# A conv-FFN encoder's last down projections: every second tile summed in a pair bank, eight PSUM banks in place of four

## The chip, the cores and the metric

The kernel runs on one core of one Trainium2 chip. The metric is the device time of one execution in microseconds (us). Three runs of the kernel before took 1843.85 to 1846.6 us, with a median of 1845.19.

The engines are named as in the profile: PE is TensorE (matmuls; PEld are its weight loads), DVE is VectorE, ACT is ScalarE, POOL is GpSimd, SP is SyncE, which issues the transfers. PSUM, in which TensorE sums its results, has eight banks; a [128, 512] tile of 32-bit floats fills one.

## The reference

Two sequences, a prompt of 256 tokens and a sample of 512, go through the same trunk of two layers, D = 1024. The kernel treats them as one array of 768 columns, prompt first.

```python
for l in range(2):
    h = rmsnorm(x, norm_g[l, 0]) * (1 + sc1) + sh1
    y = mlstm_mixer(h, ...) if l == 0 else swa_mixer(h, ...)   # sliding-window attention in layer 1
    x = x + g1 * y
    h = rmsnorm(x, norm_g[l, 1]) * (1 + sc2) + sh2
    x = x + g2 * conv_ffn(h, ffn_w_up[l], ffn_conv_w[l], ffn_conv_b[l], ffn_w_down[l])
return rmsnorm(x, final_g)

def conv_ffn(h, w_up, conv_w, conv_b, w_down):
    u = h @ w_up                          # 1024 -> 2 x 2816
    u = depthwise_conv3(u) + conv_b
    g, val = u[..., :2816], u[..., 2816:]
    return (silu(g) * val) @ w_down       # 2816 -> 1024
```

All in 32-bit floats. sh, sc and g come from a condition vector for each sequence.

## The kernel before

**Layout.** Activations lie transposed, channels on the 128 partitions and tokens along the columns. The residual x is eight row blocks c = 0 to 7 of 128 channels, held in two tiles (slab_4542 and slab_4543 in layer 0). A 32-bit product is made from three reduced-precision products: each operand is split into a high part (written by ScalarE, L260) and a low part (by VectorE, L261), and TensorE adds w_high x a_high, w_high x a_low and w_low x a_high; `mm` (L254) issues each of the three. In the names of the profile a weight's parts are whi and wlo, an activation's zh and zl.

**The conv-FFN.** `ffn` runs over NPART = 11 parts of 256 hidden channels. `up(p)` makes the part's up projection as pairs (`pair`, matmuls at L1169, L1170, L1172), which use a fixed set of four PSUM banks, `self.bank[0]` to `self.bank[3]` (tiles named ps), and ScalarE and VectorE take the results out of them (L1182, L1223, L1229, L1240, L1242, L1243). Convolution and gate follow (L1387, L1389, L1390, L1397, L1402). `down(p, g)` is issued after `up(p + 1)`: part 9's down projection stands behind the pairs of part 10, and part 10's behind nothing. So the pairs are over when the last two down projections run.

**A down tile.** `tile(w, c, rng)` makes one row block c for one range of columns: two chunks of 128 hidden channels, three matmuls each, six matmuls summed in one bank; then `resid` (L590, VectorE) reads the bank and adds it, scaled, to x. Parts 0 to 9 go over each half of the weights (c 0 to 3, then 4 to 7), and in it over the sample's 512 columns and the prompt's 256, four row blocks each: 16 tiles. Part 10 goes over three ranges of 256 columns (two of the sample, then the prompt), eight row blocks each: 24 tiles. Each tile takes its bank from `pa()`, a pool of four banks that are handed out in turn (tiles named pa); a bank is written again only when VectorE's L590 has read it.

**The norm behind part 10.** After each range the next norm begins: `square` (L111, ScalarE) of every x block, sums of the squares (L115, on POOL in layer 0 and on VectorE in layer 1), a matmul with `inv` that sums over partitions (the pm tile; in the last range of layer 1 the squares are summed by matmuls at L129), L152 or L150, a power on POOL (L153), and a matmul with `kct` (the pr tile) that spreads the factor over the partitions. Then `apply`: in layer 0 `modulated`, which makes the next layer's zh and zl (L549 on VectorE, L551 on ScalarE, L552 on VectorE) for the attention's projections; in layer 1 `output` (L574, L578, L579, L581) and the store of the result (L582). Beside it, the first projections of layer 1's attention already run on the ranges that are ready; L868 (ScalarE) and L870 (VectorE) take the first heads' results out of the ps banks, L895 and L896 others'.

**What sets the order.** The instructions of each engine are put in order by a scheduler, which lays the program out on a timeline of its own when it is built. The order of the code sets priorities, not positions. Which bank a tile has is therefore an input of the order: an instruction that would wait for a bank is placed behind others that would not. The banks of `pa()` are handed out in that scheduled order, the fixed banks by the code.

`ps()` hands out the four fixed banks in turn:

```python
def ps(self):
    if self.bank is None:
        return self.pb.tile([P, 512], F32, tag="ps", name=self.nm("ps"), bufs=4)
    self.turn += 1
    return self.bank[self.turn % 4]

def pa(self):
    return self.psp.tile([P, 512], F32, tag="pa", name=self.nm("pa"), bufs=4)
```

## Time and profile before

| | |
|---|---|
| median of three runs | 1845.19 us (1843.85 to 1846.6) |
| the profiled execution | 1843.78 us, with a span of 1842.0 us from first to last instruction |
| mean granted TensorE clock | 0.994 |
| TensorE busy | 1793.2 us, 97% of the span |
| VectorE busy | 1367.0 us, 74% |
| ScalarE busy | 895.3 us, 49% |
| POOL busy | 488.0 us, 26% |
| layer 0: parts 9 and 10 of the down projection | about 994 to 1042 us |
| layer 1: parts 9 and 10 of the down projection | about 1785 to 1832 us |

Times in the profile are counted from the start of the span. A row of the timeline gives start, duration, engine, line, operation, out<-in, sizes, count, and in brackets how long the engine had been idle and what it waited for. A row of the view of waits gives total, number and longest wait. A row of the view of windows gives each engine's busy time in a stretch, and the mean clock that TensorE was granted in it. Matmuls overlap, so a listed matmul lasts longer than the distance to the next one.

### The profile page before, as it was taken

Reading aid. Unit: us, or ns where it says so; the run is one execution under the profiler, and the core shown is the slowest. Engines: PE = TensorE matmul, PEld = TensorE weight load, DVE = VectorE, ACT = ScalarE, POOL = GpSimd, SP = SyncE. Lnnn points to the kernel's source line nnn. Section 1 sums busy time; section 2 is a strip of 40 time slices with the busy share of each in tenths; the row PEclk is TensorE's granted clock in tenths of the full one; section 3 lists DMA queues with packets and bytes.
Section 4 is the critical chain, followed back from the end, with each engine's and each line's share of the span. In section 5 each row is a group of like instructions: output and inputs, shape, how many; then the busy total and the mean of one; then the engine's idle time right before and its main releaser. Section 6 shows DMA issues by size and latency. Waiting matters only on the chain.

```text
span 1842.0 us, 28931 instructions
## 1 busy us (share of the span) xinstructions
PE 1793.2 (97%) x11290; PEld 1657.4 (90%) x11290; DVE 1367.0 (74%) x2101; ACT 895.3 (49%) x1815; POOL 488.0 (26%) x386
## 2 busy tenths in 40 slices
PE   6999999999999999999999999999999999999997
PEld 3987887889998999999999999889989999999997
DVE  4755676886689877777777757766898777777776
ACT  4443443354456444444444556765564444444443
POOL 1001001021024333333331313430144333333322
PEclk9999999999999999999999999999999999999999
DMA  8344566546312221222223321124122222222212
GB/s 330 119 145 134 172 195 221 164 138 219 101 46 74 76 61 66 69 69 69 69 69 93 104 83 50 53 94 129 50 86 69 69 69 69 69 69 70 69 35 69
DMA packets 64245, 184.48 MB, mean 100 GB/s; under 512 B 6167, under 2 KB 23831, under 8 KB 64108
## 3 DMA queue, kind: packets, MB, share of 16 engines
q1 hardware_dynamic: 64108, 182.63, 30.8%
q8 instruction: 89, 1.46, 0.3%
q14 instruction: 48, 0.39, 0.1%
HBM read 176.17 MB, written 6.43 MB: 99 GB/s over the span
## 4 chain that ended last, share of the span: by engine, by line
PE 86%; DVE 6%; DMA 3%; ACT 2%; issue 1%; POOL 1%; SPq 0%; POOLq 0%; ACTq 0%; DVEq 0%
PE ps L254 27%; PE pa L254 25%; PE ps L1169 10%; PE ps L1172 10%; PE ps L1170 10%; PE pa L1008 1%; DMA slab<-in_adaln_w_dram 1%; DMA raw<-in_w_dram 1%; DVE wlo L261 1%; DVE ada L506 1%; DVE slab L590 1%; DMA raw<-in_adaln_w_dram 0%; PE pa L1172 0%; PE pa L1169 0%; PE pa L1170 0%
## 5 line engine op out<-in xcount | busy, mean ns | idle before, releaser
L260 ACT CAST whi<-raw 128x1024 fp32r<-128x1024 f32 x237 | 247.9, 1048 | 350.4 <-PE pa L254 161.4
L261 DVE TENSOR_TENSOR wlo<-raw,whi 128x1024 fp32r<-128x1024 f32 x237 | 316.6, 1337 | 119.8 <-ACT whi L260 117.3
L254 PE MATMUL pa<-slab,whi 128*128 128x256 f32 (+1 forms) x1472 | 346.6, 331 | 3.2 <-DVE slab L590 3.2
L254 PEld LDWEIGHTS pa<-slab,whi 128*128 128x128 f32 x1472 | 252.7, 188 | 27.5 <-DVE slab L590 4.5
L590 DVE SCALAR_TENSOR_TENSOR slab<-pa,mod,slab 128x256 f32<-128x256 f32 (+1 forms) x368 | 211.2, 592 | 70.8 <-PE pa L254 70.5
L254 PE MATMUL pa<-slab,wlo 128*128 128x256 f32 (+1 forms) x736 | 233.9, 330 | 0.0
L254 PE MATMUL ps<-zh,whi 128*128 128x256 f32 (+1 forms) x560 | 189.0, 339 | 2.3 <-ACT whi L260 1.7
L254 PE MATMUL ps<-zh,wlo 128*128 128x256 f32 (+1 forms) x560 | 184.1, 330 | 2.0 <-DVE wlo L261 2.0
L254 PE MATMUL ps<-zl,whi 128*128 128x256 f32 (+1 forms) x560 | 185.1, 332 | 0.0
L1169 PE MATMUL ps<-zh,whi 128*128 128x384 f32 x504 | 172.3, 342 | 3.6 <-ACT nt L1240 1.8
L1170 PE MATMUL ps<-zl,whi 128*128 128x384 f32 x504 | 169.9, 337 | 0.8 <-DVE zl L1126 0.8
L1172 PE MATMUL ps<-zh,wlo 128*128 128x384 f32 x504 | 168.9, 335 | 0.0
L254 PEld LDWEIGHTS pa<-slab,wlo 128*128 128x128 f32 x736 | 138.5, 188 | 13.1 <-DVE wlo L261 0.4
L1205 POOL TENSOR_TENSOR raw<-raw,raw 128x512 f32<-128x512 f32 x40 | 52.2, 1305 | 330.8 <-DVE wlo L261 259.4
L254 PE MATMUL ps<-slab,whi 128*128 128x384 f32 x512 | 132.0, 339 | 0.9 <-DVE slab L261 0.5
L1402 POOL TENSOR_TENSOR slab<-slab 128x772 f32<-128x772 f32 x44 | 86.5, 1967 | 164.6 <-DVE slab L1390 152.7
L1389 DVE SCALAR_TENSOR_TENSOR slab<-slab,cstt,slab 128x771 f32<-128x771 f32 x88 | 103.6, 1179 | 26.6 <-ACT slab L1387 26.5
L254 PEld LDWEIGHTS ps<-zh,whi 128*128 128x128 f32 x560 | 107.4, 192 | 15.9 <-issue 4.4
L506 DVE SCALAR_TENSOR_TENSOR ada<-raw,silc,ada 128x1024 f32<-128x1024 f32 x84 | 110.6, 1354 | 14.9 <-DMA raw<-in_adaln_w_dram 14.8
L1202 POOL TENSOR_TENSOR raw<-raw 128x512 f32<-128x512 f32 x40 | 68.5, 1712 | 200.1 <-DMA raw<-in_w_dram 169.7
L254 PEld LDWEIGHTS ps<-zh,wlo 128*128 128x128 f32 x560 | 107.2, 192 | 12.2 <-DVE wlo L261 2.9
L254 PEld LDWEIGHTS ps<-zl,whi 128*128 128x128 f32 x560 | 107.4, 192 | 11.9 <-issue 3.4
(291 smaller groups left out, 4265.7 us busy)
## 6 DMA issues: line engine op xcount, KB each, us to landing
raw<-in_w_dram SPq DMA_DIRECT2D x208, 512.0 KB, 3.7
raw<-in_adaln_w_dram SPq DMA_DIRECT2D x84, 512.0 KB, 4.6
slab<-in_x_dram SPq DMA_DIRECT2D x12, 512.0 KB, 6.8
slab<-in_adaln_w_dram SPq DMA_DIRECT2D x12, 512.0 KB, 10.3
slab<-mrows SPq DMA_DIRECT2D x8, 384.0 KB, 5.3
xs<-slab SPq DMA_DIRECT2D x6, 512.0 KB, 3.6
bt<-brow SPq DMA_DIRECT2D x16, 192.0 KB, 3.0
slab<-xs SPq DMA_DIRECT2D x6, 512.0 KB, 6.9
```

The lines of the kernel that those rows point to most:

```text
L254: self.nc.tensor.matmul(out, lhsT, rhs, start=start, stop=stop)
L260: nc.scalar.copy(hi, src)
L261: return nc.vector.tensor_tensor(lo, src, hi.bitcast(F32), ALU.subtract)
L506: stt(acc[:, s], row, w, acc[:, s], ALU.mult, ALU.add)
L590: self.nc.vector.scalar_tensor_tensor(x, o, self.mod[l][:, gc + c, q : q + 1], x, ALU.mult, ALU.add)
L1169: mm(o, wh[:, k], hi[k], start=start and k == 0, stop=False, skip_group_check=True)
L1170: mm(o, wh[:, k], lo[k], start=False, stop=False, skip_group_check=True)
L1172: mm(o, wl[:, k], hi[k], start=False, stop=k == 3, skip_group_check=True)
L1202: tt(q[2], q[2], q[3], ALU.add)
L1205: tt(q[0], q[2], q[0], ALU.subtract)
L1389: stt(y[:, 1:], u[:, :-1], w(0), y[:, 1:], ALU.mult, ALU.add)
L1402: nc.gpsimd.tensor_tensor(y, y, yrow[:, j], ALU.mult)
```

## The change

`tile` gets a fourth argument, `more`. Where it is true, the row blocks with odd c take their bank from `ps()`, the four fixed banks of the pairs, and the others from `pa()` as before. It is true for all of part 9 (`p == NPART - 2`), and in part 10 for the first two ranges of layer 0 and for all three of layer 1 (`keep is None` is layer 1). The prompt range of layer 0 stays as it was. Both layers are concerned: eight of 16 tiles of part 9, and eight (layer 0) or twelve (layer 1) of 24 of part 10.

```diff
-            def tile(w, c, rng):
+            def tile(w, c, rng, more=False):
                 s0, s1, _ = rng
-                o = self.pa()[:, : s1 - s0]
+                o = (self.ps() if more and c % 2 else self.pa())[:, : s1 - s0]
                 cs = slice(c % 4 * P, (c % 4 + 1) * P)
...
                     for rng in SAMPLE, PROMPT:
                         for c in range(4 * h, 4 * h + 4):
-                            tile(w, c, rng)
+                            tile(w, c, rng, p == NPART - 2)
                 return
...
                 for c in range(KC):
-                    tile(ws[c // 4], c, rng)
+                    tile(ws[c // 4], c, rng, keep is None or rng is not RANGES[-1])
                     norm.square(c)
```

No instruction is added or removed. Up to the down projection of part 9 in layer 0 the order is the same; from there the orders of SP and POOL are the same, and those of TensorE, VectorE and ScalarE differ in two stretches: from that place to the start of layer 1's attention, and from the down projection of part 9 in layer 1 to the end of the program.

On TensorE, in layer 0, just ahead of the last twelve pair matmuls of part 10, stand the first matmuls of part 9's tiles (slab_8743 is the gate's result, whi_9408 the weight; 128x512 are tiles of the sample, 128x256 of the prompt). The first row of these, on pa_9412, is the same in both; the rows after it:

```order
-L254 MATMUL pa_9420<-slab_8743,whi_9408 128x512 x2
-L254 MATMUL pa_9428<-slab_8743,whi_9408 128x512 x2
-L254 MATMUL pa_9436<-slab_8743,whi_9408 128x512 x2
+L254 MATMUL pa_9427<-slab_8743,whi_9408 128x512 x2
+L254 MATMUL pa_9442<-slab_8743,whi_9408 128x256 x2
+L254 MATMUL pa_9457<-slab_8743,whi_9408 128x256 x2
+L254 MATMUL ps_4533<-slab_8743,whi_9408 128x256 x2
```

Three wide tiles on pa banks gave way to one wide and two narrow ones on pa banks and a narrow one on the pair bank ps_4533.

On VectorE, at the start of layer 1's attention, the last range's apply (L549, L552; pa_10005 in the kernel before and pa_9989 in the one after are the pr tile, slab_9926 and slab_9927 projections of the attention), before:

```order
L870 TENSOR_TENSOR slab_9926<-ps_9914,slab_9926 64x512 x2
L549 TENSOR_SCALAR nt_10008<-slab_4542,gain_92,pa_10005 128x256
L549 TENSOR_SCALAR nt_10012<-slab_4542,gain_92,pa_10005 128x256
L549 TENSOR_SCALAR nt_10016<-slab_4542,gain_92,pa_10005 128x256
L549 TENSOR_SCALAR nt_10020<-slab_4542,gain_92,pa_10005 128x256
L549 TENSOR_SCALAR nt_10024<-slab_4543,gain_92,pa_10005 128x256
L549 TENSOR_SCALAR nt_10028<-slab_4543,gain_92,pa_10005 128x256
L549 TENSOR_SCALAR nt_10032<-slab_4543,gain_92,pa_10005 128x256
L549 TENSOR_SCALAR nt_10036<-slab_4543,gain_92,pa_10005 128x256
L870 TENSOR_TENSOR slab_9927<-ps_9915,slab_9927 64x512 x2
L870 TENSOR_TENSOR slab_9926<-ps_9914,slab_9926 64x512 x2
L552 TENSOR_SCALAR zl<-nt_10008,mod_89,zh 128x256
```

and after, in the same rows of the order:

```order
L549 TENSOR_SCALAR nt_9992<-slab_4542,gain_92,pa_9989 128x256
L549 TENSOR_SCALAR nt_9996<-slab_4542,gain_92,pa_9989 128x256
L549 TENSOR_SCALAR nt_10000<-slab_4542,gain_92,pa_9989 128x256
L549 TENSOR_SCALAR nt_10004<-slab_4542,gain_92,pa_9989 128x256
L549 TENSOR_SCALAR nt_10008<-slab_4543,gain_92,pa_9989 128x256
L549 TENSOR_SCALAR nt_10012<-slab_4543,gain_92,pa_9989 128x256
L549 TENSOR_SCALAR nt_10016<-slab_4543,gain_92,pa_9989 128x256
L549 TENSOR_SCALAR nt_10020<-slab_4543,gain_92,pa_9989 128x256
L870 TENSOR_TENSOR slab_9910<-ps_9898,slab_9910 64x512 x2
L552 TENSOR_SCALAR zl<-nt_9992,mod_89,zh 128x256
L552 TENSOR_SCALAR zl<-nt_9996,mod_89,zh 128x256
L870 TENSOR_TENSOR slab_9911<-ps_9899,slab_9911 64x512 x2
```

slab_9910 and slab_9911 are the names of slab_9926 and slab_9927 in the kernel after. The two L870 ahead of the eight L549 have moved behind them; of the four that followed the L549, ahead of the first L552, two now stand behind the second L552 and two behind the last.

On VectorE, at the end of the program, from the last range's L152 on (the L581 of pa_17679 before and of pa_17645 after are the outputs of range 1, the last two rows those of the prompt range), before:

```order
L152 TENSOR_SCALAR nr_17624<-pa_17617 128x2
L590 TENSOR_SCALAR slab_12452<-pa_17655,mod_89,slab_12452 128x256
L590 TENSOR_SCALAR slab_12453<-pa_17667,mod_89,slab_12453 128x256
L581 TENSOR_SCALAR slab_12452<-slab_12452,cstt,pa_17679 128x256 x2
L581 TENSOR_SCALAR slab_12453<-slab_12453,cstt,pa_17679 128x256 x2
L590 TENSOR_SCALAR slab_12453<-pa_17689,mod_89,slab_12453 128x256
L581 TENSOR_SCALAR slab_12453<-slab_12453,cstt,pa_17679 128x256 x2
L590 TENSOR_SCALAR slab_12453<-pa_17701,mod_89,slab_12453 128x256
L590 TENSOR_SCALAR slab_12453<-pa_17718,mod_89,slab_12453 128x256
L581 TENSOR_SCALAR slab_12452<-slab_12452,cstt,pa_17747 128x256 x3
L581 TENSOR_SCALAR slab_12453<-slab_12453,cstt,pa_17747 128x256 x2
```

and after:

```order
L152 TENSOR_SCALAR nr_17592<-pa_17585 128x2
L590 TENSOR_SCALAR slab_12437<-pa_17633,mod_89,slab_12437 128x256
L581 TENSOR_SCALAR slab_12436<-slab_12436,cstt,pa_17645 128x256 x2
L581 TENSOR_SCALAR slab_12437<-slab_12437,cstt,pa_17645 128x256 x4
L590 TENSOR_SCALAR slab_12437<-pa_17666,mod_89,slab_12437 128x256
L581 TENSOR_SCALAR slab_12436<-slab_12436,cstt,pa_17711 128x256 x3
L581 TENSOR_SCALAR slab_12437<-slab_12437,cstt,pa_17711 128x256 x2
```

Three of the prompt range's L590 stood between and behind the L581 of range 1; now one does, behind all six.

## The prediction

> **What bounds the kernel now.** I read the page's shares and its chain first, then the view of waits, then the timeline of the two stretches in which the changed tiles run.

> ```profile
> core 0: 1842.0 us, clock 0.994
> PE 1793.2 (97%) x11290; PEld 1657.4 (90%) x11290; DVE 1367.0 (74%) x2101; ACT 895.3 (49%) x1815; POOL 488.0 (26%) x386
> PE 86%; DVE 6%; DMA 3%; ACT 2%; issue 1%; POOL 1%; SPq 0%; POOLq 0%; ACTq 0%; DVEq 0%
> PE pa L254 <- DVE slab L590: 3.2, 7, 0.6
> PE pa L254 <- POOL nr L153: 2.5, 4, 1.0
> PE pa L254 <- DVE zl L552: 2.2, 1, 2.2
> ```

> TensorE is busy for 97% of the span and carries 86% of the chain. No work is taken from it, so the change can only win or lose TensorE's waits. Those that a freer choice of banks touches directly are 3.2 us in seven places, 0.17% of the span: bank waits on L590, the vector instruction that reads a summed tile. Taken alone they would be too small to see (a measurement of this kernel tells 0.2%, 3.7 us, from no change). So I looked at what hangs on these waits. First the end of layer 0 and the start of layer 1 (columns: start, duration, instruction, and in brackets the idle time ahead of it and who ended it):

> ```profile
> 1004.27 0.50 PE L254 MATMUL pa<-slab,whi 128*128 128x256 f32 x2 [0.50 <-DVE slab L590]
> 1004.61 0.28 PE L254 MATMUL pa<-slab,wlo 128*128 128x256 f32 x1
> 1004.73 0.40 PE L254 MATMUL pa<-slab,whi 128*128 128x256 f32 x2
> 1004.97 0.28 PE L254 MATMUL pa<-slab,wlo 128*128 128x256 f32 x1
> 1005.80 0.50 PE L254 MATMUL pa<-slab,whi 128*128 128x256 f32 x2 [0.56 <-DVE slab L590]
> 1022.51 1.50 PE L254 MATMUL pa<-inv,nt 128*128 128x2 f32 x12 [0.26 <-POOL nt L115]
> 1030.00 0.51 PE L254 MATMUL pa<-slab,whi 128*128 128x256 f32 x2 [0.36 <-DVE slab L590]
> 1052.51 0.60 PE L254 MATMUL pa<-kct,nr 128*128 128x128 f32 x4
> 1060.17 0.43 PE L254 MATMUL pa<-zl,whi 128*128 128x256 f32 x1 [2.18 <-DVE zl L552]
> 1060.39 0.42 PE L254 MATMUL pa<-zh,wlo 128*128 128x256 f32 x1
> ```

> Two things are to be seen. A stall costs more than its bracket. Matmuls run 0.12 us apart (1004.61 to 1004.73) though each is listed as 0.28 long, so the bracket begins 0.16 late; and the first two after a stall take 0.34 us (1004.27 to 1004.61) where they take 0.24 (1004.73 to 1004.97), 0.10 more. And after the wait for zl the matmuls are 0.22 us apart. The view of windows says why (columns: length, busy time and count of PE, PEld, DVE, ACT and POOL, then granted clock, DMA share, GB/s):

> ```profile
> 1004.00:1015.00 11.00, 10.18 (x61) 8.94 (x62) 10.93 (x17) 1.89 (x2) 1.86 (x1) 1.00 0.22 70
> 1060.00:1063.80 3.80, 3.63 (x17) 3.64 (x18) 3.71 (x10) 2.39 (x8) 0.00 (x0) 0.55 0.20 50
> 1063.80:1070.00 6.20, 6.20 (x53) 6.20 (x53) 4.51 (x7) 3.63 (x7) 0.00 (x0) 1.00 0.25 76
> ```

> For 3.80 us behind that wait the granted clock is 0.55, and 1.00 after it: 3.80 x 0.45 = 1.7 us more. VectorE shows what held zl, and the tail of the program holds the other four waits on L590:

> ```profile
> 1052.24 1.38 DVE L870 TENSOR_TENSOR slab<-ps,slab 64x512 fp32r<-64x512 f32 x2 [2.81 <-ACT slab L868]
> 1053.65 3.22 DVE L549 SCALAR_TENSOR_TENSOR nt<-slab,gain,pa 128x256 f32<-128x256 f32 x8
> 1056.79 2.81 DVE L870 TENSOR_TENSOR slab<-ps,slab 64x512 fp32r<-64x512 f32 x4
> 1059.63 2.46 DVE L552 SCALAR_TENSOR_TENSOR zl<-nt,mod,zh 128x256 fp32r<-128x256 f32 x6
> 1795.35 0.50 PE L254 MATMUL pa<-slab,whi 128*128 128x256 f32 x2 [0.45 <-DVE slab L590]
> 1796.88 0.50 PE L254 MATMUL pa<-slab,whi 128*128 128x256 f32 x2 [0.56 <-DVE slab L590]
> 1820.26 0.51 PE L254 MATMUL pa<-slab,whi 128*128 128x256 f32 x2 [0.42 <-DVE slab L590]
> 1821.86 0.58 PE L254 MATMUL pa<-inv,nt 128*128 128x2 f32 x4 [0.62 <-DVE nt L115]
> 1830.63 0.51 PE L254 MATMUL pa<-slab,whi 128*128 128x256 f32 x2 [0.34 <-DVE slab L590]
> 1832.26 1.05 PE L129 MATMUL pa<-inv,nt 128*128 128x2 f32 x8 [0.31 <-ACT nt L111]
> 1834.35 0.71 PE L254 MATMUL pa<-kct,nr 128*128 128x128 f32 x4 [1.04 <-POOL nr L153]
> ```

> **The change, part by part.** It adds and removes no instruction and no transfer, and SyncE and POOL keep their order; it removes waits on banks and moves instructions on TensorE, VectorE and ScalarE in these two stretches.

> *Down projection of part 9, layer 0.* Two stalls, 0.50 and 0.56, with 0.16 + 0.10 each: 1.6 us. They go if a tile's bank is free eight tiles after its last use. VectorE is the reason for them: it is busy for 10.93 of the 11.00 us from 1004. Its rows from 1000 on, and the last release of a bank of the pairs:

> ```profile
> 998.32 0.33 PE L1172 MATMUL ps<-zh,wlo 128*128 128x384 f32 x1
> 999.47 0.54 ACT L1182 COPY slab<-ps 128x128 f32<-128x128 f32 x2
> 1000.29 1.67 DVE L261 TENSOR_TENSOR wlo<-raw,whi 128x1024 fp32r<-128x1024 f32 x1
> 1001.88 0.74 DVE L590 SCALAR_TENSOR_TENSOR slab<-pa,mod,slab 128x512 f32<-128x512 f32 x1
> 1002.54 1.01 DVE L1389 SCALAR_TENSOR_TENSOR slab<-slab,cstt,slab 128x771 f32<-128x771 f32 x1
> 1003.47 0.74 DVE L590 SCALAR_TENSOR_TENSOR slab<-pa,mod,slab 128x512 f32<-128x512 f32 x1
> ```

> A tile of 512 columns is six matmuls of 0.23 us, 1.4 us of TensorE, against about 0.66 us of VectorE for its L590 (1001.88 to 1002.54); the backlog comes from the L261, L1389 and L1390 between them, three to four us in all, some two wide tiles. Eight banks hold it; four did not. The fourth pair bank is the last to come free: TensorE leaves it at 998.3, ScalarE's copies L1182 end at 1000.0, and the first changed tile on it stands behind about 4.6 us of other tiles, at about 1002.9. That is 2.9 us to spare, so the bank itself costs nothing; the cover is those tiles. Gain 1.6.

> *Down projection of part 10, layer 0, and its norm.* The stall at 1030.00 is 0.36 + 0.26 = 0.6, the wait for the sums at 1022.51 is 0.26 + 0.16 = 0.4. Both go: range 0 runs 1.6 us ahead, and the sum matmuls stand later in TensorE's new order, behind other tiles. Against that I expect two new short waits on zl and on POOL's sums, 0.6 together (estimate from the same rows, placed by hand). Net 0.4.

> *The wait for zl and the slow clock.* In the new order the broadcast matmul (1052.51) has eight matmuls fewer ahead of it: 8 x 0.12 = 0.95, and with the 2.6 us of stalls gone it comes at about 1049.0. Its L549 group follows directly (before, an L870 pair stood ahead): 8 x 0.40 = 3.2, from 1049.6 to 1052.8. Then only one L870 pair, 1.38, and the first zl with 0.5: ready at 1054.7. TensorE needed 5.5 us from the broadcast to the wait (1052.51 to 1057.99); with the eight matmuls that moved behind the broadcast it is 6.4, so it comes at 1055.4, 0.7 us after zl. The wait of 2.2 us and the slow stretch of 1.7 go: 3.9. The later zl come every 0.4 us but for one L870 pair, and TensorE takes a new one every nine matmuls, 1.06 us, so they are in time. What is late next is wlo (L261) of the value projection, for VectorE now has four L870 behind the L552: I expect up to 0.4 there. Net 3.5. Its bounds: 0 if the wait stays, 3.9 if nothing replaces it. Sum of this seam: 1.6 + 0.4 + 3.5 = 5.5.

> The waits after 1063.8 up to the tail keep their cause (weights and casts), so the lead is carried along.

> *The tail.* The two stalls of part 9 are 0.45 + 0.56 + 0.52 = 1.5. In part 10 the stall at 1820.26 (0.7) goes, but the sums at 1821.86 still wait for VectorE's L115: the lead shrinks to nothing there. It returns with the next broadcast, which has two tiles between itself and those sums in the new order and had four: 2 x 0.70 = 1.4. At the very end VectorE does the following:

> ```profile
> 1828.53 1.65 DVE L581 SCALAR_TENSOR_TENSOR slab<-slab,cstt,pa 128x256 f32<-128x256 f32 x4 [0.81 <-ACT nt L574]
> 1830.10 0.48 DVE L590 SCALAR_TENSOR_TENSOR slab<-pa,mod,slab 128x256 f32<-128x256 f32 x1
> 1830.50 0.86 DVE L581 SCALAR_TENSOR_TENSOR slab<-slab,cstt,pa 128x256 f32<-128x256 f32 x2
> 1831.28 0.87 DVE L590 SCALAR_TENSOR_TENSOR slab<-pa,mod,slab 128x256 f32<-128x256 f32 x2
> ```

> Before, three L590 stand behind L581; now one, but behind all six (6 x 0.40 = 2.4 us). With the broadcast 1.4 earlier the six run from about 1826.9 to 1829.3, the last L590 to 1829.8, its square and sums (0.42 and some 0.9) to about 1831.2, against 1832.26 + 1.05 = 1833.3 before. What follows to the end (0.70 of L153, output, stores) is the same chain. Gain 2.1, bounds 0 (the L590 late by its 2.4) and 3.4 (every wait there on L590 gone too).

> **The sum.** 5.5 + 2.1 = 7.6. The profiled execution is its span of 1842.0 and 1.8 around it, 1843.78: it becomes about 1836.2. The median of the runs is 1.4 above the profiled one, so I forecast 1837.5, 0.4% faster; from its own bounds, 1834 to 1840.

> [...] In the down stretch above, with four banks rotated and two stalls, the granted clock is 1.00: short stalls of half a microsecond did not slow it. [...]

> **The rivals.**
> - *The wait for zl stays.* Its margin is 0.7 us, out of 10 us of VectorE work that I placed by hand. If it is lost by some two microseconds, wait and slow clock come back, 3.9: gain 3.7, at 1841.5, on the edge of what can be told. For it: VectorE is busy throughout there. Against: three L870 pairs stood ahead of zl, now one.
> - *VectorE is the bound in any case.* It is 99% busy from 1004 to 1015, so banks might only put off the stall, and the norms would lose the lead again: gain 1, 1844.2. Against: VectorE has work for less than TensorE's time over a whole part (74% of the span).
> [...]
> - *Slower: the pairs' banks come late.* A changed tile on a bank that a pair's readers still hold stops TensorE, which takes its matmuls in order. Up to 2.9 us it is hidden; beyond, each microsecond counts in both layers. It is slower by 3.7 when it costs 7.6 + 3.7 = 11.3, 5.7 in each layer: ScalarE's release would have to come 8.6 us late, as it would behind casts moved ahead of it. That gives 1849. The trace has the release 1.7 us behind the last matmul; but the order of ScalarE and VectorE is new here.

> **How the numbers follow.** Forecast 0.56, zl stays 0.20 (half of it below, half within 0.2%), VectorE bound 0.08, clock 0.04, late banks 0.12, which is more than the rows give, because so much order is new. Faster 0.56 + 0.10 = 0.66, same 0.10 + 0.08 + 0.04 = 0.22, slower 0.12. The range takes in the forecast's bounds and the first two rivals, 0.84: 1834 to 1844.3.

> **What would show it.** Right: no wait of TensorE on L590 in the part 9 stretches; the wait for zl gone and the clock at 1.00 at the start of layer 1; the last sums 2 us nearer to the start of the part. Wrong: a TensorE wait on L1182 or L1242, a slow window anywhere in the two stretches, a longer wait on L261 in the value projection, or the last L590 ending the tail.

## The result and the profile after

The changed kernel takes 1839.43 us, median of eight runs (1837.64 to 1841.57), against 1844.74 us of eight runs of the kernel before: 0.9970 of the time, with a 95% interval of 0.9962 to 0.9979. That is 5.3 us, 0.3% faster. The forecast was 1837.5, with a range of 1834 to 1844.3. (One execution of a kernel of the next section took 2186 us at a mean granted clock of 0.75; the ratios leave it out.)

The profiled execution has a span of 1837.3 us, 4.7 less than before. The page's shares, then the rows of the view of TensorE's waits (total, number, longest) that bear on the two stretches or are new:

```profile
PE 1792.4 (98%) x11290; PEld 1657.9 (90%) x11290; DVE 1373.0 (75%) x2101; ACT 893.9 (49%) x1815; POOL 486.6 (26%) x386
```

```profile
PE pa L254 <- POOL nr L153: 2.9, 4, 1.2
PE ps L1170 <- DVE zl L1126: 1.8, 5, 1.0
PE pa L129 <- ACT nt L111: 1.0, 1, 1.0
PE pa L254 <- DVE nt L115: 0.6, 1, 0.6
PE ps L254 <- DVE zl L552: 0.5, 1, 0.5
```

The waits on L590 (3.2 us in seven places) are gone altogether, and so is the wait of 2.2 us on zl; one of 0.5 us, earlier, has come in its place. Two others are new or longer: 1.0 us on the squares (L111) at the very end, and 1.0 us on zl of L1126, in the middle of layer 1 (the longest of its five there; before, its longest was 0.2).

At the seam of the layers, the timeline of VectorE and then of TensorE in the kernel after:

```profile
1049.43 3.22 DVE L549 SCALAR_TENSOR_TENSOR nt<-slab,gain,pa 128x256 f32<-128x256 f32 x8 [4.63 <-PE pa L254]
1052.57 1.37 DVE L870 TENSOR_TENSOR slab<-ps,slab 64x512 fp32r<-64x512 f32 x2
1053.98 0.88 DVE L552 SCALAR_TENSOR_TENSOR zl<-nt,mod,zh 128x256 fp32r<-128x256 f32 x2
1054.78 1.37 DVE L870 TENSOR_TENSOR slab<-ps,slab 64x512 fp32r<-64x512 f32 x2
```

```profile
997.00 0.33 PE L1172 MATMUL ps<-zh,wlo 128*128 128x384 f32 x1
1048.79 0.60 PE L254 MATMUL pa<-kct,nr 128*128 128x128 f32 x4
1054.84 0.39 PE L254 MATMUL pa<-zl,whi 128*128 128x256 f32 x1
1063.22 0.28 PE L254 MATMUL ps<-whi,zh 128*128 128x256 f32 x1
```

The broadcast comes at 1048.79, the first zl is ready at about 1054.4 and TensorE takes it at 1054.84, without a wait. The value projection (ps<-whi,zh) begins 66.2 us after the last pair matmul of layer 0 (1063.22 - 997.00); in the kernel before it was 71.7 us, from 998.32 to this row:

```profile
1070.03 0.28 PE L254 MATMUL ps<-whi,zh 128*128 128x256 f32 x1
```

So this stretch is 5.5 us shorter. The view of windows of the kernel after shows the clock at 1.00 where it was 0.55, and in the last two rows what is new in the tail:

```profile
1004.00:1015.00 11.00, 11.00 (x72) 9.96 (x72) 11.00 (x17) 2.94 (x3) 1.87 (x1) 1.00 0.15 50
1060.00:1063.80 3.80, 3.80 (x34) 3.80 (x33) 3.71 (x6) 2.00 (x4) 0.00 (x0) 1.00 0.44 133
1817.90:1821.30 3.40, 3.40 (x32) 3.40 (x32) 1.32 (x4) 1.80 (x5) 0.70 (x1) 1.00 0.33 116
1821.30:1828.00 6.70, 5.70 (x27) 5.58 (x26) 2.83 (x7) 2.43 (x6) 1.42 (x2) 0.50 0.46 156
```

From 1821.3 to the end of the span the granted clock is 0.50. In the kernel before it fell only behind the last broadcast (1834.35), at 1835.19. The tail of the kernel after, TensorE and then VectorE:

```profile
1816.67 0.38 PE L254 MATMUL pa<-inv,nt 128*128 128x2 f32 x2 [0.59 <-DVE nt L115]
1819.99 1.40 PE L129 MATMUL pa<-inv,nt 128*128 128x2 f32 x12
1821.25 1.16 PE L254 MATMUL pa<-kct,nr 128*128 128x128 f32 x4
1826.18 1.87 PE L129 MATMUL pa<-inv,nt 128*128 128x2 f32 x8 [1.00 <-ACT nt L111]
1829.09 1.22 PE L254 MATMUL pa<-kct,nr 128*128 128x128 f32 x4 [1.04 <-POOL nr L153]
```

```profile
1822.85 2.44 DVE L581 SCALAR_TENSOR_TENSOR slab<-slab,cstt,pa 128x256 f32<-128x256 f32 x6 [2.17 <-ACT nt L574]
1825.21 0.47 DVE L590 SCALAR_TENSOR_TENSOR slab<-pa,mod,slab 128x256 f32<-128x256 f32 x1
```

The same eight L129 take 1.87 us where they took 1.05, the broadcast 1.22 where it took 0.71; and the last L590 stands behind six L581, for which TensorE waits 1.0 us.

Where the 4.7 us of the two profiled executions lie, by the times of the same matmuls:

| stretch | before | after | difference |
|---|---|---|---|
| start to the last pair matmul of layer 0 | 998.32 | 997.00 | -1.3 |
| from there to the value projection of layer 1 | 71.71 | 66.22 | -5.5 |
| from there to the last pair matmul of layer 1 | 719.41 | 720.72 | +1.3 |
| from there to the last broadcast | 44.91 | 45.15 | +0.2 |
| from there to the end of the span | 7.65 | 8.17 | +0.5 |

Of the first row 0.2 us are the shorter filling matmuls ahead of the last twelve pair matmuls; the rest of it was gained ahead of the place where the two orders part. The third row is a stretch whose instructions are the same; 1.0 of its 1.3 us is the wait on L1126, which the last section takes up. So two rows belong to the change: the seam wins 5.5 us, and the tail loses 0.8.

### The profile page after: what moved, and what is told of

The parts are those of the page before. It is cut to its first block, busy times and chain, and to the rows that moved or that the text cites. A ratio compares the mean times of both kernels' runs of the same rounds, so it can differ in the third digit from the quotient of the medians.

```text
span 1837.3 us, 28927 instructions
## 1 busy us (share of the span) xinstructions
PE 1792.4 (98%) x11290; PEld 1657.9 (90%) x11290; DVE 1373.0 (75%) x2101; ACT 893.9 (49%) x1815; POOL 486.6 (26%) x386
## 4 chain that ended last, share of the span: by engine, by line
PE 87%; DVE 5%; DMA 3%; ACT 2%; issue 1%; POOL 1%; SPq 0%; POOLq 0%; ACTq 0%; DVEq 0%
PE ps L254 29%; PE pa L254 24%; PE ps L1169 10%; PE ps L1172 10%; PE ps L1170 10%; PE pa L1008 1%; DMA slab<-in_adaln_w_dram 1%; DMA raw<-in_adaln_w_dram 1%; DMA raw<-in_w_dram 1%; DVE wlo L261 1%; DVE ada L506 1%; PE pa L1169 0%; PE pa L1172 0%; PE pa L1170 0%; DMA slab<-mrows 0%
## 5 line engine op out<-in xcount | busy, mean ns | idle before, releaser
L260 ACT CAST whi<-raw 128x1024 fp32r<-128x1024 f32 x237 | 247.9, 1048 | 344.2 <-PE pa L254 145.6
L261 DVE TENSOR_TENSOR wlo<-raw,whi 128x1024 fp32r<-128x1024 f32 x237 | 321.7, 1358 | 112.9 <-ACT whi L260 110.5
L254 PE MATMUL pa<-slab,whi 128*128 128x256 f32 (+1 forms) x1328 | 317.2, 334 | 0.0
L254 PEld LDWEIGHTS pa<-slab,whi 128*128 128x128 f32 x1328 | 230.2, 189 | 21.8 <-DVE slab L590 0.2
L590 DVE SCALAR_TENSOR_TENSOR slab<-pa,mod,slab 128x256 f32<-128x256 f32 (+1 forms) x332 | 192.8, 598 | 65.1 <-PE pa L254 65.0
L254 PE MATMUL pa<-slab,wlo 128*128 128x256 f32 (+1 forms) x664 | 212.7, 333 | 0.0
L254 PE MATMUL ps<-zh,whi 128*128 128x256 f32 (+1 forms) x560 | 189.2, 339 | 2.2 <-ACT whi L260 1.6
L254 PE MATMUL ps<-zh,wlo 128*128 128x256 f32 (+1 forms) x560 | 183.9, 330 | 1.7 <-DVE wlo L261 1.7
L254 PE MATMUL ps<-zl,whi 128*128 128x256 f32 (+1 forms) x560 | 185.0, 333 | 0.5 <-DVE zl L552 0.5
L1172 PE MATMUL ps<-zh,wlo 128*128 128x384 f32 x504 | 168.9, 335 | 0.0
L254 PE MATMUL ps<-slab,whi 128*128 128x384 f32 (+2 forms) x656 | 163.1, 332 | 0.9 <-DVE slab L261 0.5
L1205 POOL TENSOR_TENSOR raw<-raw,raw 128x512 f32<-128x512 f32 x40 | 52.0, 1299 | 331.0 <-DVE wlo L261 246.4
L254 PEld LDWEIGHTS pa<-slab,wlo 128*128 128x128 f32 x664 | 125.2, 189 | 12.6 <-DVE wlo L261 0.4
L1389 DVE SCALAR_TENSOR_TENSOR slab<-slab,cstt,slab 128x771 f32<-128x771 f32 x88 | 104.6, 1190 | 26.7 <-ACT slab L1387 26.5
L254 PEld LDWEIGHTS ps<-zh,whi 128*128 128x128 f32 x560 | 107.4, 192 | 15.8 <-issue 4.4
L254 PEld LDWEIGHTS ps<-zl,whi 128*128 128x128 f32 x560 | 107.4, 193 | 12.7 <-issue 3.4
L254 PEld LDWEIGHTS ps<-slab,whi 128*128 128x128 f32 x656 | 115.1, 188 | 3.4 <-ACT whi L260 0.9
```

The source lines that it names most:

```text
L254: self.nc.tensor.matmul(out, lhsT, rhs, start=start, stop=stop)
L260: nc.scalar.copy(hi, src)
L261: return nc.vector.tensor_tensor(lo, src, hi.bitcast(F32), ALU.subtract)
L590: self.nc.vector.scalar_tensor_tensor(x, o, self.mod[l][:, gc + c, q : q + 1], x, ALU.mult, ALU.add)
L1172: mm(o, wl[:, k], hi[k], start=False, stop=k == 3, skip_group_check=True)
L1205: tt(q[0], q[2], q[0], ALU.subtract)
```

## The experiments

Two theories stood against each other. A: the gain is made at the seam, and hangs on the order of VectorE around the wait for zl; the tail gives nothing. B: the gain is that of the bank stalls, in both layers. For the tail: C, the early fall of the clock is chance; D, it comes from the order of the work; E, from TensorE's waits alone. In the diffs, + is against the changed kernel unless said otherwise; l is the layer.

**Layer 0 alone.**

```diff
-                            tile(w, c, rng, p == NPART - 2)
+                            tile(w, c, rng, p == NPART - 2 and l == 0)
...
-                    tile(ws[c // 4], c, rng, keep is None or rng is not RANGES[-1])
+                    tile(ws[c // 4], c, rng, keep is not None and rng is not RANGES[-1])
```

> The change in layer 0 alone, the tail of the program as before. Theory A (the gain is made at the seam of the two layers: bank stalls of part 9, then the wait for zl and the slow clock behind it; the tail of the changed kernel gives nothing because its sums are bunched and its clock falls early): 5 to 6 us faster than before, as fast as the changed kernel or up to 1 us faster, no TensorE wait on zl of L552 over 0.6 us, clock 1.00 from 1056 to 1070. Rival B (the gain is that of the bank stalls, spread over both layers): about 2.6 us faster, half of the whole gain.

1840.39 us; 0.9973 of before (0.9961 to 0.9985). It is as fast as the changed kernel, within the noise, with the change in one of the two layers. From the last pair matmul to the value projection it takes 66.2 us, and its tail that of before, 44.9 us to the last broadcast. Its view of windows has the clock at 1.00 in both places:

```profile
1056.00:1063.80 7.80, 7.80 (x64) 7.65 (x64) 7.63 (x15) 4.97 (x12) 0.00 (x0) 1.00 0.27 78
1820.00:1830.00 10.00, 8.31 (x71) 8.06 (x70) 4.85 (x13) 4.51 (x11) 2.82 (x4) 1.00 0.27 90
```

B, which wanted about 2.6 us from each layer, falls.

**Layer 1 alone.**

```diff
-                            tile(w, c, rng, p == NPART - 2)
+                            tile(w, c, rng, p == NPART - 2 and l == 1)
...
-                    tile(ws[c // 4], c, rng, keep is None or rng is not RANGES[-1])
+                    tile(ws[c // 4], c, rng, keep is None)
```

> The change in layer 1 alone. Theory A: between 1 us faster and 1 us slower than before, although no TensorE wait on L590 is left in the part 9 stretch of layer 1; the granted clock is near 0.5 from about the second broadcast of the tail to the end, where the kernel before has 1.00; the 2.2 us wait for zl at the seam stays. Rival B: about 2.6 us faster. Rival C (the early fall of the clock in the tail is chance, by where a free-running window lies): the clock stays at 1.00 up to the last broadcast and the kernel is 1 to 2 us faster.

1845.61 us; 1.0001 (0.9991 to 1.0011): no difference that can be told. The wait on zl is 2.2 us, the stretch to the value projection 71.7 us. No wait on L590 is left in the tail, and still nothing is won as a whole. The clock falls in the tail here too, by this row of the windows from 1829.5, 6 us ahead of the last broadcast (1835.30):

```profile
1829.50:1836.00 6.50, 5.08 (x25) 4.91 (x24) 2.83 (x7) 2.54 (x7) 2.10 (x3) 0.50 0.47 161
```

In this execution the tail to the last broadcast was 43.9 us, 1.0 less than before: the low clock came later in it, by the work, than in the changed kernel's.

**Part 9 alone, and part 10 alone, in both layers.**

```diff
-                    tile(ws[c // 4], c, rng, keep is None or rng is not RANGES[-1])
+                    tile(ws[c // 4], c, rng)
```

> Part 9 alone, in both layers; part 10 keeps its four banks. VectorE's order at the seam is then that of before (a pair of L870 ahead of the eight L549, four L870 ahead of the first L552), and the sums of the tail are spread between tiles as before. Theory A: the part 9 stalls go (1.6 us in each layer), the wait for zl and the slow stretch stay: 2.5 to 3.5 us faster, clock 1.00 in the tail up to the last broadcast. Rival B: nearly the whole gain, 4.5 to 5.5 us.

```diff
-                            tile(w, c, rng, p == NPART - 2)
+                            tile(w, c, rng)
```

> Part 10 alone, in both layers; part 9 keeps its four banks. VectorE's order at the seam is that of before, the sums of the tail are bunched as in the changed kernel. Theory A: the stalls of part 9 and the wait for zl stay, the tail loses to the low clock what it wins: between 1 us faster and 1.5 us slower. Rival B: about 1 us faster. Rival C (low clock by chance): clock 1.00 up to the last broadcast.

Part 9 alone: 1844.36 us, 0.9998 (0.9986 to 1.0009). That is less than either theory wanted. The wait on zl stays, as A said; but the bank stalls were not won either. They have moved into part 10, which has four banks, as TensorE's timeline shows (0.79 and 1.00 us with what a stall costs beside its bracket), and the stretch to the value projection is 71.5 us:

```profile
1019.02 0.51 PE L254 MATMUL pa<-slab,whi 128*128 128x256 f32 x2 [0.53 <-DVE slab L590]
1031.82 0.39 PE L254 MATMUL pa<-slab,whi 128*128 128x256 f32 x1 [0.74 <-DVE slab L590]
```

A's other expectation for this kernel, a clock of 1.00 in the tail up to the last broadcast, failed in the profiled execution (1850.95 us, 6.6 above the median of this kernel). Its sums stand in the tail mostly in fours between tiles, as before, and yet the clock fell at 1824.0, behind a wait of 1.4 us on L115, and stayed down to the end; the tail to the last broadcast took 50.0 us for 44.9:

```profile
1824.00:1841.00 17.00, 15.96 (x77) 15.88 (x75) 5.41 (x13) 4.77 (x12) 2.80 (x4) 0.50 0.20 68
```

So an early fall does not need the changed order of the tail.

Part 10 alone: 1850.14 us, 1.0023 (1.0011 to 1.0035), slower. Here something had not been thought of. In its profiled execution (1846.21 us, 3.9 below the median of this kernel) the wait of 2.2 us on zl was there, from 1058.9 to 1061.0, and the clock did not fall behind it:

```profile
1055.91:1059.33 3.42, 2.93 (x16) 1.64 (x15) 3.38 (x8) 3.38 (x9) 0.00 (x0) 1.00 0.00 0
1059.33:1062.74 3.41, 1.72 (x14) 1.72 (x15) 3.37 (x8) 3.17 (x10) 0.00 (x0) 1.00 0.04 10
```

A second profile of the same kernel shows more.

> A second profile of the kernel with part 10 alone on eight banks, whose median was 5 us above before while its profiled execution, the fastest of twelve, was not. If the rest is slow clock, this execution has more stretches at clock 0.5 than the first (which had four, the last from 17 us before the end), each of 3.4 us; if it is a wait, the view of waits shows one of several us that the first had not.

1850.01 us. The waits are the same, 2.2 us on zl and 1.5 us on L115 in the tail among them; but this time the clock fell behind the wait on zl, and once more at 1029. The first row holds most of the wait (1061.5 to 1063.7), at full clock still; the others hold the two slow stretches:

```profile
1059.86:1063.28 3.42, 1.64 (x6) 0.53 (x5) 3.33 (x7) 3.40 (x9) 0.00 (x0) 1.00 0.00 0
1029.00:1033.00 4.00, 4.00 (x23) 4.00 (x22) 2.22 (x6) 2.19 (x6) 2.73 (x4) 0.57 0.38 131
1063.00:1067.00 4.00, 3.33 (x16) 3.33 (x17) 3.90 (x10) 2.90 (x9) 0.00 (x0) 0.57 0.14 34
```

Added up in windows of 1 us, each of these slow stretches takes 1.71 us of clock (3.41 us at 0.50): the same instructions, with the same waits, may or may not pay it. Which it is can be read from the traces. In each of the fourteen profiles of this study, the places where the clock changes lie whole multiples of 3.413 us from each other (in the kernel before it falls at 1060.37 and at 1835.19, 774.82 us or 227 times 3.413 apart); the rows of 3.41 and 3.42 us above are cut on these grids. In the first profile a boundary of the grid, 1059.33, fell into the wait, and 16 and 14 matmuls ran in the windows on its two sides; in the second most of the wait lay in one window with only 6, and the clock fell at that window's end.

No wait of several us is new in the second profile, and it has three slow stretches more than the first (six against three in all; the new ones are at 152, 1029 and 1063), so slow clock is what sets these two executions apart. The tail took 47.0 us to the last broadcast in this execution and 47.1 in the first, 2.1 and 2.2 more than before; why the typical time is 5 us above before, stretch by stretch, two profiles don't settle.

**Which tiles matter at the seam: the same number, another order.** In layer 0 alone, part 9 and one range of part 10, the first or the second: twelve tiles on the pairs' banks in both. With the first the scheduler leaves VectorE's order at the seam as it was; with the second it makes that of the changed kernel.

```diff
-                    tile(ws[c // 4], c, rng, keep is None or rng is not RANGES[-1])
+                    tile(ws[c // 4], c, rng, RANGES.index(rng) in ((0,), ())[l])      # first range
...
+                    tile(ws[c // 4], c, rng, RANGES.index(rng) in ((1,), ())[l])      # second range
```

> Layer 0 alone, part 9 and of part 10 only the first range (12 tiles on the pairs' banks). VectorE's order at the seam stays that of before (the broadcast at the same place among TensorE's matmuls, one pair of L870 ahead of the L549, two pairs ahead of the first L552). Theory A (the gain hangs on the order around the wait for zl, which only some choices of banks bring about): the wait of 2.2 us for zl stays, at most 1.5 us faster than before. Rival B (the gain is that of the bank stalls of part 9): about the gain of the kernel changed in layer 0 alone, 4 to 5.5 us.

> Layer 0 alone, part 9 and of part 10 only the second range: as many tiles moved as in the run before it, but the order at the seam is that of the changed kernel (the broadcast seven matmuls earlier, both L870 pairs behind the L549). Theory A: no TensorE wait of over 0.8 us on zl between 1050 and 1065, clock 1.00 there, 4 to 6 us faster than before. Rival B: like the run with the first range.

First range: 1844.91 us, 0.9996 (0.9986 to 1.0006). Second range: 1842.35 us, 0.9982 (0.9971 to 0.9992). The view of TensorE's waits from 994 to 1070 and VectorE's timeline, with the first range:

```profile
PE pa L254 <- DVE zl L552: 2.2, 1, 2.2
PE pa L254 <- POOL nt L115: 1.2, 1, 1.2
```

```profile
1054.22 3.22 DVE L549 SCALAR_TENSOR_TENSOR nt<-slab,gain,pa 128x256 f32<-128x256 f32 x8
1057.36 2.81 DVE L870 TENSOR_TENSOR slab<-ps,slab 64x512 fp32r<-64x512 f32 x4
1060.20 2.46 DVE L552 SCALAR_TENSOR_TENSOR zl<-nt,mod,zh 128x256 fp32r<-128x256 f32 x6
```

and with the second:

```profile
PE pa L254 <- POOL nr L153: 1.1, 1, 1.1
```

```profile
1053.33 3.22 DVE L549 SCALAR_TENSOR_TENSOR nt<-slab,gain,pa 128x256 f32<-128x256 f32 x8 [3.73 <-PE pa L254]
1056.46 1.37 DVE L870 TENSOR_TENSOR slab<-ps,slab 64x512 fp32r<-64x512 f32 x2
1057.87 0.88 DVE L552 SCALAR_TENSOR_TENSOR zl<-nt,mod,zh 128x256 fp32r<-128x256 f32 x2
```

The stretch to the value projection is 71.5 us with the first range and 67.7 with the second, though the second paid 1.71 us of slow clock in it, from 1027 to 1032, behind its new wait of 1.1 us on POOL. With the same number of tiles moved, the gain goes with the order. (No run forces the new order with four banks, which would part the two entirely.) The second missed the expected 4 us: 2.9 by the medians. In its profiled execution the slow stretch and 1.2 us more than before behind the last pair matmul of layer 1, where the instructions are those of before, account for that.

**All three ranges in layer 0.**

```diff
-                    tile(ws[c // 4], c, rng, keep is None or rng is not RANGES[-1])
+                    tile(ws[c // 4], c, rng, RANGES.index(rng) in ((0, 1, 2), ())[l])
```

(part 9 in layer 0 only, as above)

> Layer 0 alone, part 9 and all three ranges of part 10 (the prompt range is the one that the change leaves out). The broadcast stands 14 matmuls earlier than before and four L552 ahead of the second L870 pair. Theory A: the same 4 to 6 us as with two ranges, since nothing is left to win at the seam once zl is in time and the clock stays up; up to 1 us more if short waits on L552 and POOL go too.

1845.62 us, 0.9999 (0.9988 to 1.001). Nothing is left of the gain: more tiles on eight banks are not better, and the expected 4 to 6 us did not come. Zl is in time, but other waits have come, 1.2 us on L590 and 2.3 us on the wlo of the value projection, and a slow stretch at 1048, in the view of waits from 994 to 1075 and of windows:

```profile
PE ps L254 <- DVE wlo L261: 2.3, 2, 1.8
PE pa L254 <- DVE slab L590: 1.2, 1, 1.2
```

```profile
1047.00:1052.00 5.00, 5.00 (x32) 5.00 (x31) 3.34 (x9) 1.27 (x3) 0.00 (x0) 0.66 0.56 178
```

**Other tails.** Layer 0 as changed; in layer 1 part 9 with the second range of part 10, and then with the first two.

```diff
-                    tile(ws[c // 4], c, rng, keep is None or rng is not RANGES[-1])
+                    tile(ws[c // 4], c, rng, RANGES.index(rng) in ((0, 1), (1,))[l])      # second range
...
+                    tile(ws[c // 4], c, rng, RANGES.index(rng) in ((0, 1), (0, 1))[l])    # first two
```

> Layer 0 as in the changed kernel; in layer 1 part 9 and of part 10 only the second range. In the tail the sum matmuls stand between tiles as before, not bunched, and three L590 stand among the L581. Theory A (the tail of the changed kernel loses because the prompt range's tiles on the pairs' banks bunch the sums and put the last L590 behind six L581): faster than the changed kernel by 1 to 3 us, 6 to 8 us faster than before, clock 1.00 to within 9 us of the end. Rival C (the tail's low clock is chance): no faster than the changed kernel.

> The changed kernel without the prompt range of layer 1: there part 9 and the first two ranges of part 10 use eight banks, as in layer 0. The sums of the tail stand between tiles, not bunched, but the second broadcast comes ahead of the last three tiles and the L590 of the last three stand behind six L581. Theory A: the seam's gain of 5.5 us stays, the clock stays at 1.00 to within 9 us of the end, the tail gains 0 to 2 us: 5 to 7 us faster than before. Rival C (the tail's clock falls by chance alone): like the changed kernel.

1840.29 us, 0.9977 (0.9962 to 0.9992), and 1842.19 us, 0.9982 (0.9973 to 0.9991). The seam takes 66.2 us in both, so that part of A holds again; both missed on the tail. The sums stand between tiles, but the waits have moved onto the sums: 1.6 us on L115 and 1.2 on L153 in the one (44.9 us to the last broadcast, as before), 3.5 us on L115 in the other (46.8 us). In the tail's view of waits of the second:

```profile
PE pa L254 <- DVE nt L115: 3.5, 1, 3.5
```

Behind that wait the clock fell for 3.41 us, from 1816.5 on, so the expected 1.00 failed there too. (The profiled execution took 1838.80 us, 3.4 below the median of this kernel.) A's reason for the tail, that only the prompt range's tiles do harm, falls.

**What the clock goes by.** The matmuls with which the norms behind part 10 of layer 1 sum their squares multiply by a constant of two equal columns. Here they multiply by 64 equal columns, of which one is read. The order of TensorE is that of the changed kernel; at the end of VectorE's, the last L590 stands behind four L581 and ahead of two, as in the kernel with layer 1 alone.

```diff
-        self.wait = wait
-        self.pm = None
+        self.wait, self.w = wait, 64 if apply == net.output else 2
+        self.pm, self.ones = None, lambda: net.inv if self.w == 2 else net.inv[:, :1].to_broadcast([P, self.w])
...
-                    o, self.sums[i][:, b * P : (b + 1) * P], self.net.inv,
+                    o, self.sums[i][:, b * P : (b + 1) * P], self.ones(),
```

(the same for the other sums of these norms, at L254, and the columns of pm that are written and read, 64 apart)

> The changed kernel, but the matmuls that sum the squares in the norms behind part 10 of layer 1 (L129, and those with inv) stream 64 equal columns in place of 2; the order of TensorE and the banks are the same. It asks what the clock goes by. Theory D (the clock falls in the tail because its bunched two-column matmuls hardly use the array, though TensorE counts as busy): a matmul of 64 columns lasts as long as one of 2 columns in the trace (0.11 us, within 0.03), the clock stays at 1.00 until the wait ahead of the last broadcast in most executions, the last pair matmul is 1.5 to 2 us nearer to the last broadcast than in the changed kernel (45.7 us), and the kernel is 1 to 2 us faster than the changed one. Theory E (the clock goes by TensorE's waits alone, 0.6 and 1.0 us here): the clock falls as in the changed kernel, same time.

1836.76 us in five executions; 0.9955 of before (0.9942 to 0.9969), the fastest of all: 8.0 us below before and, by the medians, 2.7 below the changed kernel. The two were not run side by side, and their intervals overlap a little, so the 2.7 is less sure than the traces of the tail. The tail of TensorE and its windows:

```profile
1819.67 1.45 PE L129 MATMUL pa<-inv,nt 128*128 128x64 f32 x12
1820.95 0.66 PE L254 MATMUL pa<-kct,nr 128*128 128x128 f32 x4
1824.61 1.10 PE L129 MATMUL pa<-inv,nt 128*128 128x64 f32 x8 [1.45 <-ACT nt L111]
1826.75 0.95 PE L254 MATMUL pa<-kct,nr 128*128 128x128 f32 x4 [1.03 <-POOL nr L153]
```

```profile
1817.40:1820.80 3.40, 3.40 (x33) 3.40 (x32) 1.51 (x5) 1.99 (x6) 0.70 (x1) 1.00 0.38 132
1820.80:1827.00 6.20, 3.71 (x31) 3.44 (x31) 2.83 (x7) 2.61 (x8) 2.11 (x3) 1.00 0.45 151
```

Twelve sums start over 1.28 us (1819.67 to 1820.95), as twelve of two columns did (1819.99 to 1821.25): 0.11 us each. The clock stays at 1.00 up to the last broadcast, though TensorE now waits longer there, 1.45 us for 1.00. The last pair matmul is 43.1 us from the last broadcast, 2.0 less than in the changed kernel (45.15, not the 45.7 of the expectation) and 1.8 less than before. E falls, since the waits are no shorter. D stands for this tail: in the four profiles with the sums bunched and two columns wide (the changed kernel, layer 1 alone, and part 10 alone twice) the clock fell 6 to 9 us ahead of the last broadcast. C is right in part, as part 9 alone showed: where the grid lies over the work has its share. All executions, not only the profiled ones, say the same of this tail: the median of their mean granted clocks is 0.993 with layer 0 alone as well as before, 0.990 with layer 1 alone, 0.9915 for the changed kernel, and 0.995 with the wide sums. Not all of the 2.0 is clock: up to two L581, 0.8 us, is the place of the last L590. Against the kernel with layer 1 alone, which has the same order in its tail, it is 43.1 to 43.9, there with a fall of the clock that came late.

**The wide sums in the kernel before.** The same edit with four banks throughout; the order of every engine is that of before.

> The kernel before, with four banks throughout, and the sums of 64 columns in the norms behind part 10 of layer 1; the order of every engine is that of before. Theory D (the wide sums only keep the clock up where the changed kernel's bunched sums let it fall): in the tail of before the clock is at 1.00 anyway until after the last broadcast, so the time is that of before within 1 us, and from the last pair matmul to the last broadcast 44.9 us. If the wide sums win by themselves (less waiting, another cause), it is 2 to 3 us faster.

1844.97 us; 1.0002 (0.9993 to 1.0011). The wide sums by themselves win nothing: they only keep what the changed order would lose.

## Why the prediction was right, and where not

The time lies in the range, 1.9 us above the number. Of the two terms of the sum, the seam came out as forecast; the tail was wrong in its sign, by 2.9 us of a forecast gain of 7.6. The range "from its own bounds, 1834 to 1840" does not follow from the bounds given: with 0 to 3.9 for the wait and 0 to 3.4 for the tail the gain is 2.0 to 9.3 us, which makes 1835.9 to 1843.2.

*The seam: 5.5 forecast, 5.5 measured.* The steps came in the order in which they had been placed, and zl was ready 0.4 us ahead of TensorE where 0.7 had been worked out. The broadcast at about 1049.0 was at 1048.79, but this agreement is luck: this execution had reached the seam 1.3 us earlier. Counted from the last pair matmul of layer 0, the broadcast came at 51.8 us where 50.7 had been placed, and TensorE took the first zl at 57.8 where 57.1 had been placed. The total held because about as much had been set aside for new waits (0.6) and for wlo (0.4). The pairs' last bank was first used 4.8 us behind the last pair matmul (4.6 forecast) without a wait, so the rival of late banks did not come. New waits were 0.5 us on zl and 0.3 on L153, with 0.6 forecast; the 0.4 us on wlo did not come.

*What the split of that term missed.* Part 9's 1.6 us was booked as won by its eight banks. Part 9 alone wins 0.2 us in this stretch: the stalls come back in part 10. The rival that VectorE is the bound and banks only put off the stall was right for part 9 alone. And the larger piece, 3.9 us for the wait and the slow clock, was booked as the consequence of the lead; the pair of kernels with twelve tiles each shows that it goes with the order, which the scheduler finds for some choices of banks and not for others. That order had been read before the forecast, and the wait on zl was rightly taken from it; that the pieces add up to 5.5 so exactly is in part luck.

*The slow stretch of 1.7 us is not certain.* It was subtracted as if it always followed the wait of 2.2 us. Of the seven profiles with that wait six have it; one and the same kernel had it in one profile and not in the other. Each slow stretch at the seam is 3.41 us at 0.50, and the grid of 3.413 us lies differently over the work in each profile: a boundary at 1059.33 in the first profile of part 10 alone and at 1059.86 in the second. TensorE was not idle in the 3.41 us ahead of the slow stretch at the seam: it was busy for 1.2 to 1.6 us of them in those six profiles (1.23 in the kernel before, from 1056.95 to 1060.37), and for all of the 3.40 ahead of the fall in the changed kernel's tail. What the fall went with was how many columns the matmuls moved, as the last section shows.

*The tail: 2.1 forecast, 0.8 lost.* This is the step that failed: the measured loss lies outside the bounds of "Gain 2.1, bounds 0 ... and 3.4". The work was placed well enough: with the clock held up by the wide sums, the last sums ended 42.1 us behind the last pair matmul of layer 1, where 41.8 had been placed, and the tail to the last broadcast is 1.8 us shorter than before. In the changed kernel they ended at 44.1, later than before (43.9). But "What follows to the end ... is the same chain" was not true, since the chain ran at half clock. The prediction looked at the clock for the down stretches only, and for short waits; it did not ask what a stretch of bunched two-column sums does to it. Two of its signs of being wrong did come: a slow window in one of the two stretches, and the last L590, behind six L581, holding back the last sums. To a falling clock the forecast gives 0.04, its author's estimate. In the changed kernel the clock did fall, at 1821.3 in the tail, behind the bunched sums; from 1004 to 1015 it is at 1.00 with eight banks as with four.

*The waits on L590* went to nothing, as forecast for part 9; that their 3.2 us in themselves were worth little was right too: layer 1 alone removed its four and won nothing as a whole.

## What to carry to other kernels

A wait of half a microsecond on a bank may matter less for itself than for the order it brings about; look in the new order for what stands ahead of the instruction that ends the longest wait nearby, and price that. Where small reductions on TensorE are gathered into a bunch, read the granted clock there, not the busy time, and give them more columns as long as their duration does not grow (here they start 0.11 us apart with 64 columns as with two). One profile can show a slow stretch that the next lacks (six of the seven with the wait of 2.2 us had it), so a slow stretch is priced by its share of the executions, not in full. And where a stretch is fed by one busy engine, more buffers there may only move the stall into the stretch behind, as with part 9 alone, where 0.79 and 1.00 us came back in part 10.

## What the runs showed of the hardware

*Two instructions of VectorE took 1.1 us longer in one profile than in another, beside POOL, in the same code.* In the stretch in the middle of layer 1 that is the same in both kernels, two L1126 took 1.22 us in the kernel before and 2.32 in the one after, where POOL's L1205 began beside the second of them (1.66 us for 0.56). VectorE's timeline, before and then after:

```profile
1336.22 1.22 DVE L1126 TENSOR_TENSOR zl<-slab,zh 128x384 fp32r<-128x384 f32 x2
```

```profile
1329.88 2.32 DVE L1126 TENSOR_TENSOR zl<-slab,zh 128x384 fp32r<-128x384 f32 x2
```

POOL's timeline in the kernel after:

```profile
1330.51 1.28 POOL L1205 TENSOR_TENSOR raw<-raw,raw 128x512 f32<-128x512 f32 x1 [22.93 <-ACT zh L1120]
```

In the kernel before, the same L1205 began at 1337.11, 0.3 us ahead of the end of the two. TensorE waited 1.0 us for it. POOL's L1205 itself took no longer, 1.28 us for 1.48. The kernels with layer 0 alone and with layer 1 alone, the latter with that stretch and all ahead of it as before, lost the same microsecond there, and the others did not, the one with the wide sums among them; so it is not put down to the change. That POOL's instruction held VectorE's up is read from the times alone; no run takes one of the two away, so it is not shown.
